# One pool of eight PSUM banks, three score groups in a run, and new step orders in a ragged attention kernel

## The chip, the cores and the metric

The kernel runs on one core of a Trainium2 chip. The metric is the device time in microseconds (us) of one execution. The core has five engines with a queue each: TensorE (PE, matrix products; the load of its weights is listed as PEld), VectorE (DVE), ScalarE (ACT), GpSimd (POOL) and SyncE (SP, which issues the transfers here). The engines wait for each other through semaphores only. PE writes its products to PSUM, a memory of eight banks, each of 512 fp32 values on 128 partitions; DVE or ACT must read a bank out before PE may write it again.

## The reference

32 sequences of up to 512 rows; each has its own length, drawn between 64 and 511, and eight heads of 64.

```python
output = np.zeros_like(x)
for b in range(batch):
    seq_len = lengths[b]
    x_b = x[b, :seq_len].copy()
    qkv = np.matmul(x_b, w_qkv)
    q, k, v = np.split(qkv, 3, axis=-1)        # then 8 heads of 64
    scores = scale * np.matmul(q, k.transpose(0, 2, 1))
    attn = np.exp(scores - np.max(scores, axis=-1, keepdims=True))
    attn = attn / (np.sum(attn, axis=-1, keepdims=True) + 1e-08)
    output[b, :seq_len] = np.matmul(attn, v).transpose(1, 0, 2).reshape(seq_len, dim)
```

## The kernel before

A head sorts the 32 sequences on the chip by length, longest first, and projects the first one. Then come seven loops, for padded lengths N of 512, 448, 384, 320, 256, 192 and 128. A loop's iteration handles two sequences, called **positions** j = 0 and j = 1; each has its own set of buffers. In this draw the loops run 1, 1, 4, 2, 3, 3 and 2 iterations, so 2, 2, 8, 4, 6, 6 and 4 positions. The number n of row tiles of 128 is 4 for 512 and 448, 3 for 384 and 320, 2 for 256 and 192, 1 for 128.

A position does the attention of its own sequence and, between that, the projections of the sequence of the next position (buffer index `o = 1 - j`). The work is written as **steps**, and the string `ORDER[N]` (lines 201 to 211) is the program order of every engine:

- `S` is a run of score groups. A group (`scores`, line 885) is PE's products of K and Q for two heads, in the upper and lower 64 rows of the array, into two adjacent banks (line 901), and ACT's exp of both banks into an fp16 tile `et` (line 915). For n = 4 there are 16 groups, for n = 3 there are 12, for n = 2 four, for n = 1 one. PE's group is emitted as the op `s…`; the ACT ops of a run come behind all PE groups of the run.
- `Q`, `K`, `V` (lines 926 and 949): four matmuls of full 128 rows per bank (more and narrower ones for lengths that are no multiple of 128; for N = 192 and 256 one Q or K step covers two column blocks), then a copy to fp16 by DVE, or by ACT where the step has a star.
- `A` (line 961): the product of `et` and the values with a column of ones (line 974) into one bank, then three DVE instructions: reciprocal `R` (line 984), masking of the reciprocal `U` (line 987), division `O` into the output tile (line 995). The bank is free when `O` has read it. For n = 4 an `A` step covers one head, for n = 3 and n = 2 two heads, for n = 1 four.
- `P`: mask (DVE, line 806), casts of a later sequence (POOL), its load (SP). `L`: the column of ones (DVE). `X`: SP's transposing transfer of the cast sequence, which is read two positions later. The store comes at the end of each position.

Before the change the banks are in two sets. `s_bufs` has two pairs, used in turn by the score groups, so a run is of two groups at most: a third would wait for the exp of the first. `singles` has four banks, dealt out in rounds of four or three by `ring_of` (line 781) to the Q, K, V and A steps in the order of `ORDER`.

`plan_waits` (line 35) follows the ops in program order and derives each op's waits from what it reads and writes (`bk3`, `ps0`, `et1` and so on). An order or a bank that is changed thus changes the waits; it needs no other edit. A wait stands ahead of its instruction in its engine's queue, and holds what is behind it.

Of the kernel before, what the change touches and what calls it, by code (L numbers as in the profile page):

```python
# [17 lines left out]
P = 128  # L18
# [16 lines left out]
def plan_waits(head, bodies, entries):  # L35
# [11 lines left out]


    waits = defaultdict(list)
    has = [{op.name for j in range(2) for op in body[j]} for body in bodies]  # L50
    shared = set().union(*has)

    def follow(chain):
# [4 lines left out]
        for at, v in enumerate(chain):  # L58
# [10 lines left out]
            for w, j, k, op in todo:  # L69
# [8 lines left out]
                for r in op.writes:  # L78
                    needs += [(o, False) for o in readers[r]]
                    needs += [(write[r], False)] if r in write else []  # L80
                for wait in waits[w, j, k]:
                    got = [
                        o
                        for o in seen[wait[1]]
                        if wait[0] in ("last", "entry", "head", "lead")
                        or (wait[0] == "pos" and o["b"] == b - wait[2])
                        or (wait[0] == "iter" and o["b"] // 2 == b // 2 - wait[2])
                        or (wait[0] == "posin" and o["b"] == first - wait[2])
                        or (wait[0] == "iterin" and o["b"] // 2 == first // 2 - wait[2])
                    ]  # L90
                    if got:
                        learn(got[-1])
# [53 lines left out]
def kernel(  # L146
# [25 lines left out]
    def ring(n, shape, dtype, name, pool=const):  # L172
# [11 lines left out]
    e_bufs = ring(4, [P, 2 * NT * MAXS], F16, "et")  # L184
    r_bufs = ring(4, [P, 2 * NT], FP32, "rcp")
    zeros = const.tile([P, NT - 1, D], FP32)
    order_i = const.tile([P, B + 8], I32)
    alive = const.tile([P, B + 8, NT], FP32)

    s_bufs = ring(2, [P, 2 * BANK], FP32, "psc", pool=ps)  # L190
    singles = ring(4, [P, BANK], FP32, "bank", pool=ps)

# [6 lines left out]
    LOOPS = [512, 448, 384, 320, 256, 192, 128]  # L199

    ORDER = {
        512: "P L S0 K2* Q1 S1 V0 K0 S2 A0 K1 S3 Q3* A1 S4 Q0 K3 S5 V3* Q2 S6 A2 A3 V2 S7 V1 X A4 "
        "A5 A6 A7",
        448: "P L S0 Q0 V3 S1 Q1* K0 S2 K2 V0 S3 K3 Q2 S4 A0 A1 A2 S5 K1 Q3 S6 A3 A4 A5 S7 V2 V1 X "
        "A6 A7",
        384: "P L S0 K0 V0* S1 V1 Q0* S2 A0 V2* S3 Q1 K1* A2 S4 Q2 Q3 S5 A4 K3 K2* X A6",
        320: "P L S0 K0* V0* S1 Q1 V1 S2 A0 V2 S3 A2 K1 Q0 S4 Q2* Q3* S5 A4 K3* K2* X A6",
        256: "P L V1* V0 S0 Q0* Q2 A0 S1 K2 A2 A4 K0* X A6",
        192: "P L S0 V0* V1 K0 S1 Q2 A0 Q0* A2 A4 K2* X A6",
        128: "P L S0 K0* Q0 V0 X A0 A4",  # L210
# [57 lines left out]
    def before_loops():  # L268
# [146 lines left out]
        hit_i = hit("hit_i", idx_f, idc_f, ("idx_f", "idc_f"))  # L415
        sorted_i = spread("phit_i", hit_i, singles[2], "bk2", 0)
        hit_l = hit("hit_l", idx_f, lenc_f, ("idx_f", "lenc_f"))
        sorted_l = spread("phit_l", hit_l, singles[1], "bk1", 0)
        op(
# [44 lines left out]
        back_l = hit("back_l", idr_f, lenc_f, ("idr_f", "lenc_f"))  # L464
        mirrored_i = spread("pback_i", back_i, singles[3], "bk3", 0)
        mirrored_l = spread("pback_l", back_l, singles[3], "bk3", B)

# [113 lines left out]
        def cast_tile(b, t, eng):  # L581
# [7 lines left out]

        where = {f"bk{k}": singles[k] for k in range(4)}  # L590
        where |= {
            f"ps{k}.{h}": s_bufs[k][:, h * BANK : (h + 1) * BANK] for k in range(2) for h in range(2)
        }

# [45 lines left out]
        def warm():  # L640
            for k in range(WARM):
                nc.tensor.matmul(where["ps1.1"][:, 0:P], ident16, ident16, start=True, stop=True)

        op("warm", "PE", warm, ("ident16",), ("ps1.1",))
        cast_tile(0, 0, "DVE")
        cast_tile(0, 1, "ACT")
        turn(0, 0, "ps0.0", "DVE")
        turn(0, 1, "ps0.1", "ACT")
        cast_tile(0, 2, "DVE")
        cast_tile(0, 3, "POOL")  # L650
        step("V0", "bk0", "DVE")
        turn(0, 2, "ps1.0", "DVE")
        shorten("wq", w_q, 0, 0, "ACT")
        step("V1", "bk1", "DVE")
        turn(0, 3, "ps1.1", "ACT")
        shorten("wq", w_q, 0, 1, "POOL")
        step("V2", "ps0.0", "DVE")
        shorten("wq", w_q, 0, 2, "ACT")
        step("V3", "ps0.1", "ACT")
        shorten("wq", w_q, 0, 3, "POOL")  # L660
# [12 lines left out]
        cast_tile(1, 2, "POOL")  # L673
        step("Q3", "ps1.0", "ACT")
        op(
# [45 lines left out]
        read_ends("PE", 1)  # L721
        step("K0", "ps1.1", "DVE")
        cast_tile(1, 1, "DVE")
        step("K1", "bk0", "ACT")
        cast_tile(1, 3, "ACT")
# [17 lines left out]
        )  # L743
        step("K2", "bk1", "DVE")
        for t, (bank, eng) in enumerate(
            (("ps0.0", "DVE"), ("ps0.1", "ACT"), ("ps1.0", "DVE"), ("ps1.1", "ACT"))
        ):
            turn(1, t, bank, eng)
# [31 lines left out]

    def ring_of(count):

        threes = -count % 4
        rounds = [3] * threes + [4] * ((count - 3 * threes) // 4)
        return [k for r in rounds for k in range(r)]

    def position(N, j, at, ring):
# [97 lines left out]
        def scores(g):  # L885
            group = groups[g]
            buf = g % 2 if len(groups) > 1 else j
            psc, W = s_bufs[buf], len(group) * n128
            i0, kt0 = group[0]
# [6 lines left out]
            def matmuls():  # L896
                for x, (i, kt) in enumerate(group):
                    for par in range(2):
                        r = slice(HD * par, HD * (par + 1))
                        c0 = par * BANK + x * n128  # L900
                        last = nc.tensor.matmul(  # L901
                            psc[:, c0 : c0 + N],
                            kT[r, i, kt * P : (kt + 1) * P],
                            qz[r, i, 0:N],
                            start=True,
                            stop=True,
                        )
                return last

            def exps():  # L910
                et = e_bufs[e][:, used : used + 2 * W].rearrange(
                    "p (j x q) -> p j x q", j=2, q=n128
                )
                got = psc.rearrange("p (j c) -> p j c", c=BANK)[:, :, 0:W]
                return nc.scalar.activation(  # L915
# [6 lines left out]
            reads = {f"kT{j}.{i}" for i, _ in group} | {f"qz{j}.{i}" for i, _ in group}  # L922
            op(f"s{g}", "PE", matmuls, (*sorted(reads), f"kTd{j}"), (f"ps{buf}",))
            return Op(f"S{g}", "ACT", exps, (f"ps{buf}",), (f"et{e}",))

        def qk(name, m0, is_q, act):
            k = ring.pop(0)
            bank = singles[k]
            ms = slice(m0, m0 + gm)
# [19 lines left out]
        def val(name, t, act):  # L949
            k = ring.pop(0)  # L950
            bank = singles[k]

# [8 lines left out]
        def av(h0):  # L961
            k = ring.pop(0)
            pav = singles[k][:, 0 : heads * n * (HD + 1)].rearrange(
                "p (g t d) -> p g t d", t=n, d=HD + 1
# [52 lines left out]
        for step in ORDER[N].split():  # L1017
# [10 lines left out]
            elif kind == "S":  # L1028
                run = [scores(g) for g in range(2 * num, min(2 * num + 2, len(groups)))]
                ops.extend(run)  # L1030
# [38 lines left out]
    for N in LOOPS:  # L1069
        steps = [s for s in ORDER[N].split() if s[0] in "QKVA"]  # L1070
        ring = ring_of(2 * len(steps))
        bodies.append([position(N, j, at, ring) for j in range(2)])
# [181 lines left out]
```

## Time and profile before

| | us |
|---|---|
| median of 3 runs (362.82, 363.5, 363.8) | 363.5 |
| the profiled execution's own time | 364.13 |
| its span, first to last instruction | 362.3 |
| PE busy in the span | 347.1 (96%) |
| ACT busy | 269.3 (74%) |
| DVE busy | 220.1 (61%) |

By stage, from the trace: where each loop's first PE instruction starts, and how long it lasts.

| stage | from | to | us | positions |
|---|---|---|---|---|
| head | 0 | 24.0 | 24.0 | |
| 512 | 24.0 | 63.4 | 39.4 | 2 |
| 448 | 63.4 | 99.8 | 36.4 | 2 |
| 384 | 99.8 | 205.4 | 105.6 | 8 |
| 320 | 205.4 | 254.0 | 48.6 | 4 |
| 256 | 254.0 | 300.3 | 46.3 | 6 |
| 192 | 300.3 | 340.9 | 40.6 | 6 |
| 128 | 340.9 | 362.3 | 21.4 | 4 |

In the profile's lines, a group is given by line, engine and operation, with output and inputs by the program's names. Behind the bar stand its busy time and the mean duration of one, then the idle time of the engine ahead of it, with what ended it. Matmuls overlap, so the mean duration of one is longer than the distance from one to the next. `issue` means that nothing which the profile shows was waited for.

### The profile page before, as it was taken

To read this page: it belongs to the slowest core of one execution; us is meant where nothing else is said; L and a number is where in the kernel's file an instruction comes from. 1 tells how busy PE (TensorE), PEld (TensorE's weight loads), DVE (VectorE), ACT (ScalarE), POOL (GpSimd) and SP (SyncE) were. 2 spreads that over 40 slices of the span, in tenths; PEclk is the share of its full clock that TensorE was granted. 3 is DMA by queue.
4 is the path that set the end of the run, shared out by engine and by line. 5 is a ranking of instruction groups with operands and counts; after the bars stand their busy time and mean duration, and the time that the engine had idled before them with its cause. 6 is when DMAs were issued, how large, how long until landed. Compare 5 with 4: busy or idle time off the path is not lost.

```text
span 362.3 us, 11181 instructions
## 1 busy us (share of the span) xinstructions
PE 347.1 (96%) x4274; PEld 216.1 (60%) x4274; DVE 220.1 (61%) x679; ACT 269.3 (74%) x390; POOL 96.6 (27%) x117
## 2 busy tenths in 40 slices
PE   4999999999999999999999999999999999999983
PEld 3444545474645555555555676677667777787762
DVE  4465656686856545645645666445665667667674
ACT  4379797878788898898898887888667776676541
POOL 4474040404033033033023023311223222322321
PEclk9999999999999999999999999999999999999998
DMA  5978971577169276376466469484786585875821
GB/s 202 346 255 246 261 261 24 171 277 238 55 209 299 89 225 238 103 257 197 121 243 206 128 237 249 133 267 153 239 183 213 192 250 161 259 246 185 235 75 59
DMA packets 74140, 72.35 MB, mean 200 GB/s; under 512 B 44160, under 2 KB 44160, under 8 KB 74112
## 3 DMA queue, kind: packets, MB, share of 16 engines
q1 hardware_dynamic: 74064, 71.98, 62.5%
q8 instruction: 17, 0.28, 0.3%
q14 instruction: 11, 0.09, 0.1%
q10 hardware_dynamic: 48, 0.00, 0.0%
HBM read 27.80 MB, written 33.55 MB: 169 GB/s over the span
## 4 chain that ended last, share of the span: by engine, by line
PE 91%; DMA 3%; SPq 2%; DVE 1%; issue 1%; ACT 0%
PE bank L219 39%; PE bank L230 19%; PE psc L901 16%; PE bank L974 16%; DMA w_q<-in_w_qkv_dram 2%; DMA xT<-x 1%; DMA row<-in_lengths_dram 1%; SPq L820 1%; PE psc L219 0%; SPq L487 0%; DVE v_aug L954 0%; SPq L845 0%; PE psc L230 0%; PE psc L600 0%; DVE out_nat L995 0%
## 5 line engine op out<-in xcount | busy, mean ns | idle before, releaser
L915 ACT ACTIVATE et<-psc 128x768 f16<-128x768 f32 (+3 forms) x260 | 208.4, 855 | 46.9 <-PE psc L901 46.6
L219 PE MATMUL bank<-xT,w_r 128*128 128x384 f16 (+4 forms) x1432 | 157.2, 258 | 1.4 <-DMA xT<-x 1.0
L257 POOL TENSOR_TENSOR x<-x_nat,mask 128x512 f16<-128x512 f32 x87 | 88.3, 1040 | 253.6 <-DVE mask L806 246.0
L219 PEld LDWEIGHTS bank<-xT,w_r 128*128 128x128 f16 x1432 | 99.2, 98 | 52.0 <-issue 18.7
L230 PE MATMUL bank<-w_r,xT 128*128 128x512 f16 x328 | 82.7, 382 | 0.3
L974 PEld LDWEIGHTS bank<-v_aug,et 128*128 128x128 f16 x1792 | 63.9, 98 | 14.1 <-issue 9.1
L974 PE MATMUL bank<-v_aug,et 128*128 128x65 f16 x1792 | 71.7, 194 | 0.0
L901 PE MATMUL psc<-qz,kT 64*128 64x384 f16 (+6 forms) x640 | 68.5, 306 | 1.0 <-ACT kT L939 1.0
L995 DVE TENSOR_TENSOR out_nat<-bank,rcp 128x256 f32<-128x256 f32 (+1 forms) x136 | 64.1, 472 | 4.6
L939 DVE CAST qz<-bank 128x384 f16<-128x384 f32 (+3 forms) x60 | 35.4, 591 | 40.6 <-PE bank L219 39.3
L984 DVE RECIPROCAL rcp<-bank 128x4 f32<-128x4 f32 (+1 forms) x136 | 24.7, 182 | 40.1 <-PE bank L974 40.0
L954 DVE CAST v_aug<-bank 128x512 f16<-128x512 f32 x46 | 31.8, 692 | 24.5 <-PE bank L230 24.3
L230 PEld LDWEIGHTS bank<-w_r,xT 128*128 128x128 f16 x328 | 27.8, 98 | 31.1 <-issue 6.8
L901 PEld LDWEIGHTS psc<-qz,kT 64*128 64x128 f16 x640 | 23.4, 93 | 33.1 <-issue 27.4
L939 ACT CAST kT<-bank 128x384 f16<-128x384 f32 (+2 forms) x46 | 23.1, 502 | 15.1 <-PE bank L219 15.1
L939 DVE CAST kT<-bank 128x384 f16<-128x384 f32 (+3 forms) x46 | 27.4, 595 | 7.7 <-PE bank L219 7.6
L987 DVE TENSOR_TENSOR rcp<-rcp,v_aug 128x4 f32<-128x4 f32 (+1 forms) x136 | 22.9, 169 | 4.7
L954 ACT CAST v_aug<-bank 128x512 f16<-128x512 f32 x34 | 20.0, 590 | 7.3 <-PE bank L230 6.7
L939 ACT CAST qz<-bank 128x384 f16<-128x384 f32 (+3 forms) x32 | 15.6, 502 | 2.5 <-PE bank L219 2.2
L806 DVE TENSOR_SCALAR mask<-alive 128x4 f32 x32 | 5.6, 175 | 5.7 <-issue 5.7
L869 DVE TENSOR_SCALAR v_aug<-alive 128x24 f16 (+3 forms) x32 | 7.2, 224 | 0.0
L409 PE MATMUL bank<-h_hit_i,h_ones 32*128 32x32 f16 x1 | 0.2, 204 | 4.3 <-DVE h_hit_i L392 4.3
(76 smaller groups left out, 54.9 us busy)
## 6 DMA issues: line engine op xcount, KB each, us to landing
x_nat<-in_x_dram SPq DMA_DIRECT2D x12, 768.0 KB, 4.7
out_dram<-out_nat SPq DMA_DIRECT2D x12, 768.0 KB, 3.5
x_nat<-in_x_dram SPq DMA_DIRECT2D x7, 1024.0 KB, 6.0
x_nat<-in_x_dram SPq DMA_DIRECT2D x13, 512.0 KB, 3.7
out_dram<-zeros SPq DMA_DIRECT2D x12, 512.0 KB, 5.7
out_dram<-out_nat SPq DMA_DIRECT2D x12, 512.0 KB, 3.2
out_dram<-out_nat SPq DMA_DIRECT2D x4, 1024.0 KB, 4.3
out_dram<-zeros SPq DMA_DIRECT2D x4, 768.0 KB, 8.4
```

Source lines behind the costliest of these rows:

```text
L219: last = nc.tensor.matmul(dst[:, t0 * P : t0 * P + (t1 - t0) * width], w_r[:, c, w0 : w0 + P], xT[:, t0:t1, c, 0:width], start=(c == 0), s ...
L230: last = nc.tensor.matmul(pv, xT[:, t, c, :], w_r[:, c, 2 * D : 3 * D], start=(c == 0), stop=(c == NC - 1),)
L257: return engine.tensor_tensor(out=x16, in0=x32, in1=live.broadcast_to([P, D]), op=ALU.mult)
L869: return nc.vector.tensor_scalar(out=v_bufs[o][:, 0:n, :, HD], in0=alive[:, bass.ds(at("DVE") + (j + 1), 1), 0:n] .rearrange("p o t -> p ( ...
L901: last = nc.tensor.matmul(psc[:, c0 : c0 + N], kT[r, i, kt * P : (kt + 1) * P], qz[r, i, 0:N], start=True, stop=True,)
L915: return nc.scalar.activation(out=et[:, :, :, 0:N], in_=got.rearrange("p j (x q) -> p j x q", q=n128)[:, :, :, 0:N], func=AF.Exp, scale=scale,
L939: return copy_on(act)(out=buf[:, ms, 0:N], in_=bank[:, 0 : gm * N].rearrange("p (m q) -> p m q", q=N),)
L954: return copy_on(act)(out=v_bufs[o][:, t, :, 0:HD], in_=bank.rearrange("p (h d) -> p h d", d=HD))
L974: last = nc.tensor.matmul(pav[:, g, qt, :], e_bufs[e][:, c0 + qt * P : c0 + (qt + 1) * P], v_aug[:, kt, h, :], start=(kt == 0), stop=(kt = ...
L984: return nc.vector.reciprocal(out=rcp, in_=pav[:, :, :, HD])
L987: return nc.vector.tensor_tensor(out=rcp, in0=rcp, in1=v_aug[:, 0:n, h0 : h0 + heads, HD].rearrange("p t g -> p g t"), op=ALU.mult,)
L995: return nc.vector.tensor_tensor(out=o_t[:, 0:n, h0 * HD : (h0 + heads) * HD].rearrange("p t (g d) -> p g t d", d=HD), in0=pav[:, :, :, 0:HD],
```

## The change

Four edits belong together.

1. The two sets of banks become one tile of eight banks. `allotted(N)` gives every step its bank, by a fixed rule that is worked out when the kernel is built: the banks are kept in order of their last use; a Q, K, V or A step takes the longest unused one; a score group takes the adjacent pair whose more recently used bank is oldest. It goes through both positions of a loop up to six times, until the order repeats, and keeps the last deal.
2. A run of scores has up to three groups for n = 4 and n = 3 (`RUN`), and two as before for n = 2. So a position has six runs (3, 3, 3, 3, 3, 1) in place of eight for n = 4, and four in place of six for n = 3.
3. `ORDER` is new for every length but 128. Steps change place, and stars move: some copies go from ACT to DVE and back.
4. Around it: eight reciprocal tiles in place of four, other bank names in the head, and one more dependency in `plan_waits`: an op waits for the last op of the same name, where that ran on another engine.

No matmul, exp, copy or transfer is added or removed.

```diff
-    r_bufs = ring(4, [P, 2 * NT], FP32, "rcp")
+    r_bufs = ring(8, [P, 2 * NT], FP32, "rcp")
...
-    s_bufs = ring(2, [P, 2 * BANK], FP32, "psc", pool=ps)
-    singles = ring(4, [P, BANK], FP32, "bank", pool=ps)
+    psum = ps.tile([P, 8, BANK], FP32, name="banks")
+    banks = [psum[:, k, :] for k in range(8)]
...
+    RUN = {4: 3, 3: 3, 2: 2, 1: 2}
     ORDER = {
-        512: "P L S0 K2* Q1 S1 V0 K0 S2 A0 K1 S3 Q3* A1 S4 Q0 K3 S5 V3* Q2 S6 A2 A3 V2 S7 V1 X A4 "
-        "A5 A6 A7",
-        448: "P L S0 Q0 V3 S1 Q1* K0 S2 K2 V0 S3 K3 Q2 S4 A0 A1 A2 S5 K1 Q3 S6 A3 A4 A5 S7 V2 V1 X "
-        "A6 A7",
-        384: "P L S0 K0 V0* S1 V1 Q0* S2 A0 V2* S3 Q1 K1* A2 S4 Q2 Q3 S5 A4 K3 K2* X A6",
-        320: "P L S0 K0* V0* S1 Q1 V1 S2 A0 V2 S3 A2 K1 Q0 S4 Q2* Q3* S5 A4 K3* K2* X A6",
-        256: "P L V1* V0 S0 Q0* Q2 A0 S1 K2 A2 A4 K0* X A6",
-        192: "P L S0 V0* V1 K0 S1 Q2 A0 Q0* A2 A4 K2* X A6",
+        512: "P L S0 V3 K3 Q2* S1 V2 K0 Q1 S2 Q3 K1* V0 S3 K2 A0 V1* S4 A1 Q0 X A2 S5 A3 A4 A5 A6 A7",
+        448: "P L S0 K3 K2 Q0 S1 V2 V3 A0 S2 V1 Q2 A1 S3 V0 K1 Q3* S4 K0 A2 A3 S5 Q1* X A4 A5 A6 A7",
+        384: "P L S0 Q0* K1 Q1 S1 Q3 V1 A0 S2 A2 V2 K0* S3 Q2 K2* K3* A4 A6 V0 X",
+        320: "P L S0 K2 Q1 K0 S1 V0 V2* A0 S2 K1* K3* A2 Q0* S3 Q3* A4 Q2* V1* X A6",
+        256: "P L V1* V0 S0 Q0 K2* S1 A0 K0* A2 A4 Q2* X A6",
+        192: "P L V0 S0 K0 S1 Q2 V1 A0 K2* A2 A4 A6 Q0* X",
         128: "P L S0 K0* Q0 V0 X A0 A4",
     }
...
+                needs += [(o, False) for o in seen[op.name][-1:] if o["by"] != op.eng and not op.dma]
...
-        step("K0", "ps1.1", "DVE")
+        step("K0", "bk1", "DVE")
...
-        step("K1", "bk0", "ACT")
+        step("K1", "bk2", "ACT")
...
-    def ring_of(count):
-
-        threes = -count % 4
-        rounds = [3] * threes + [4] * ((count - 3 * threes) // 4)
-        return [k for r in rounds for k in range(r)]
+    def runs(N):
+
+        groups = NH // 2 * tiles(N) // max(1, BANK // (tiles(N) * P))
+        return [min(RUN[tiles(N)], groups - k) for k in range(0, groups, RUN[tiles(N)])]
+
+    def allotted(N):
+
+
+        takes = []
+        for step in 2 * ORDER[N].split():
+            if step[0] == "S":
+                takes += [2] * runs(N)[int(step[1:])]
+            elif step[0] in "QKVA":
+                takes.append(1)
+        ages = list(range(8))
+        for _ in range(6):
+            before, got = list(ages), []
+            for n in takes:
+                first = ages[0]
+                if n == 2:
+                    first = min(
+                        range(7),
+                        key=lambda k: (
+                            max(ages.index(k), ages.index(k + 1)),
+                            ages.index(k) + ages.index(k + 1),
+                        ),
+                    )
+                got.append(first)
+                used = list(range(first, first + n))
+                ages = [k for k in ages if k not in used] + used
+            if ages == before:
+                break
+        return got
...
-            buf = g % 2 if len(groups) > 1 else j
-            psc, W = s_bufs[buf], len(group) * n128
+            k0 = ring.pop(0)
+            psc, W = [banks[k0], banks[k0 + 1]], len(group) * n128
...
-                got = psc.rearrange("p (j c) -> p j c", c=BANK)[:, :, 0:W]
+                got = psum[:, k0 : k0 + 2, 0:W]
...
-                run = [scores(g) for g in range(2 * num, min(2 * num + 2, len(groups)))]
+                first = sum(runs(N)[:num])
+                run = [scores(g) for g in range(first, first + runs(N)[num])]
```

## The prediction, made before the changed kernel ran

> **What bounds the kernel now.** I read the page first (busy shares, the chain that ended last), then the waits, then the list of groups by shape, then the timeline of the places that the change touches.
>
> ```profile
> PE 347.1 (96%) x4274; PEld 216.1 (60%) x4274; DVE 220.1 (61%) x679; ACT 269.3 (74%) x390; POOL 96.6 (27%) x117
> ...
> PE 91%; DMA 3%; SPq 2%; DVE 1%; issue 1%; ACT 0%
> ...
> PEld psc L901 <- issue: 27.4, 68, 0.6
> ...
> PEld bank L230 <- DVE out_nat L995: 0.8, 4, 0.2
> ...
> PEld bank L219 <- DVE v_aug L954: 0.7, 2, 0.4
> ```
>
> PE is the bound: 91% of the chain, and hardly a wait of PE's for a bank is listed (0.8 and 0.7 us). So time can be gained only by what PE itself does, and lost by every new wait of PE's.
>
> ```profile
> L219 PE MATMUL bank<-xT,w_r 128*128 128x384 f16 x320 | 61.2, 327 | 0.0
> ...
> L901 PE MATMUL psc<-qz,kT 64*128 64x384 f16 x192 | 23.9, 328 | 0.0
> ...
> 101.85 0.50 PE L901 MATMUL psc<-qz,kT 64*128 64x384 f16 x4
> ...
> 102.28 1.04 PE L230 MATMUL bank<-w_r,xT 128*128 128x512 f16 x4
> ```
>
> A position at N = 384 takes 13.20 us on PE (105.6 us of the stage by 8). Its blocks, start to start in the timeline: a Q or K 0.65, a V 0.865, an A 0.55. That is 8 x 0.65 + 3 x 0.865 + 4 x 0.55 = 10.0; the six runs of two groups get 3.2, or **0.535 a run**. Inside a run the second group comes 0.17 behind the first (a run is busy 23.9 / 48 = 0.50, one matmul lasts 0.33). So 2 x 0.17 of a run are its groups, and about 0.2 is paid at its two ends: the block ahead takes 0.10 longer than elsewhere (0.96 against 0.865 for the V ahead of the run at 101.85), and the run's last group 0.26 in place of 0.17. The waits show the same place: 27.4 us of weight loads of L901 that idle for nothing shown.
>
> **The change part by part.**
>
> *Longer runs.* A run of three costs 0.535 + 0.17 = 0.71, if the third group follows as the second does (bounds: 0.16, its columns alone, and 0.26, the last of a run; I take 0.17, the row of the same kind). Four such runs take 2.84 in place of 6 x 0.535 = 3.21: 0.37 less a position at N = 384. At 320 the same sum gives 0.36 (run of two 0.48, third group 0.145), at 448 and 512 about 0.39, as two of eight pairs of ends go. By itself: 8 x 0.37 + 4 x 0.36 + 4 x 0.39 = **6.0 us less**.
>
> *The bank waits that this buys.* I dealt out the banks by the rule and laid the blocks end to end, each with its readers on DVE and ACT behind it. In the middle of the positions the banks come back in time, narrowly: at 384, S1 and S2 find their banks free 0.2 to 0.5 before they ask, S3's last pair (A2 and V2 had it) 0.15. The end of a position is another matter. The reader of an A step is long, and DVE takes one at a time:
>
> ```profile
> 62.85 0.17 DVE L984 RECIPROCAL rcp<-bank 128x4 f32<-128x4 f32 x1
> ...
> 63.26 0.42 DVE L995 TENSOR_TENSOR out_nat<-bank,rcp 128x256 f32<-128x256 f32 x1
> ...
> 63.39 0.55 PE L901 MATMUL psc<-qz,kT 64*128 64x448 f16 x4
> ...
> 63.60 0.17 DVE L984 RECIPROCAL rcp<-bank 128x4 f32<-128x4 f32 x1
> ...
> 64.75 0.42 DVE L995 TENSOR_TENSOR out_nat<-bank,rcp 128x256 f32<-128x256 f32 x1
> ...
> 184.29 0.20 DVE L984 RECIPROCAL rcp<-bank 128x6 f32<-128x6 f32 x1 [1.04 <-PE bank L974]
> ...
> 184.73 0.56 DVE L995 TENSOR_TENSOR out_nat<-bank,rcp 128x384 f32<-128x384 f32 x1
> ```
>
> Reciprocals follow each other by 0.75 (62.85 to 63.60) while PE makes an A in 0.49, and the last of four ends at 65.18, 1.79 after PE began the next position at 63.39. Before, score groups had banks of their own and did not care. Now S0 takes six of eight banks at once, and the A steps at the end hold some of them.
>
> - **384, each position:** it ends A4 A6 V0, and S0's third pair is the banks of A4 and A6. From A4's start: its reciprocal at +0.76 (183.53 to 184.29), its division done at +1.75, A6's done at +2.66, free at +2.71. PE is at the next S0 after 2 x 0.55 + 0.865 + 0.095 = 2.06, at the third group after 2.41. Wait 0.30. Of 0.37 gained 0.07 to 0.08 is left: 8 x -0.08 = **-0.65**.
> - **448 to 384, once:** the loop's first deal does not know what the last loop left. S0's first pair is the bank of A6 (its division ends 1.04 after S0's nominal start, as at 64.43), the second that of A7 (+1.79). The third group then comes at 2.01 in place of 0.65: **+1.35**.
> - **512 and 448:** S0's second or third pair is A4's and A5's, and the first K or V takes A6's bank. 512 ends with five A steps behind a short S5, 448 with four. Laid out: 512 gains 0.55 in its first position (0.39, and a wait of 0.2 in S4 that the new order lacks); its second gains 0.55 and gives back 0.47; 448's first gives back 0.58 of 0.38, its second 0.3. **-0.65 and +0.1**.
> - **320:** ends V1* X A6, so only a Q1 waits for A6 (0.04) and Q3 for A2 (0.05): 4 x -0.27, +0.3 at its start for 384's A6, -0.2 at its end, where the last A6 stood 0.25 longer than others: **-0.95**.
> - **256 and 192**, runs of two as before. The 256 position is 7.72 a piece (46.3 / 6), its blocks make 7.49; the rest is a wait of V1 for A4's division (the row of L230 above), and the loop's end. New: V1's and V0's banks are A2's and A4's with Q2 and A6 in between, so it is gone, 0.1 to 0.2 a position; and 192 now opens with V0, which hides 256's last copies, where S0 waited 0.5. **-0.95** with 0.13 left at each loop end. At 192 (blocks 6.52, now 6.67) the wait of K2 for a bank goes (-0.15 each), but DVE gets one more copy (V0) and three A steps in a row: 3 x 0.75 behind A0's puts A6's division 1.6 into the next position, where, in every j = 0 but the first, S0's second group wants its bank at 1.14: 2 x +0.45. Its last position ends A6 Q0* in place of K2* A6, and the 128 loop's S0 needs that copy (340.90 is 0.93 behind K2's block), so A6's 0.25 no longer lies in that wait. **+0.2**.
> - **128:** K0 waited for V0's copy (344.85, 352.92: the row of L219). With eight banks it takes one long free; the first of the two is followed by a transfer's wait anyway (1.05 us at 349.31), the second is not: **-0.25**.
> - **Head:** K0 now uses Q2's bank, whose copy ends 0.05 after PE gets there (19.53): **+0.05**. The new dependency by name orders an op against one in an earlier loop, done tens of us before: 0, and below 0 is excluded.
> - **SP, POOL.** X comes later at 384 and 192 (behind the last block instead of ahead of A6) and earlier at 512. What it brings is read two positions later, so 6.5 us at least are there for its 1.3 to 1.6 of issue and 2.4 of transfer, also with the 1.5 us that SP was late at 334.75. The store behind it waits for the last division. POOL's casts hang on the mask behind it on DVE, up to 0.5 later, with 8 us spare. In the 512 stage, ACT's fullest (33.96 busy of 39.36), the new order has as many starred copies as the old, three. All at 0; if X's cover is gone, it costs once per position what it is late.
>
> Sum: 0.05 - 0.65 + 0.1 - 0.65 + 1.35 - 0.95 - 0.95 + 0.2 - 0.25 = **-1.75**. The profiled execution, 364.13 with a span of 362.3, lies 0.63 above the median, so its sum is 362.4; against the median, 363.5 - 1.75, about **361.8**. Bounds of this case: no wait at the ends of positions 512 to 320 and 0.1 less per third group would give 357.5; half a wait more in each n = 3 and n = 4 position (0.15 x 16) 364.1.
>
> **The rivals.**
>
> *The banks are free in time: the whole gain comes.* Then each position is its blocks: 384 -3.0, 512 and 448 -1.9, 320 -1.65, 256 -1.0, 192 -0.65, 128 -0.25, in all -8.5: **355.0**. For it: the old PE has next to no bank waits. Against it: DVE's 0.75 and 0.9 per A are measured, and the deal puts S0 on those banks.
>
> *ACT becomes late, slower than before.* ACT must do three exps behind each other (0.71 apart at 384, 0.92 at 512), and copies with a star stand behind them; the next run's banks hang on those copies. At 512, S3.2 takes K1*'s bank with 0.08 to spare and S4.1 follows S3.2's exp with none; at 320, S3.2 takes K1*'s and K3*'s with 0.13. If ACT is one exp later than I laid out, 512 and 448 pay 0.9 and 0.8 per position, 320 pays 0.5: 1.8 + 1.6 + 1.9 = 5.3 on top of -1.75, **367.0**; it decides for slower from 2.8 us, half an exp. For it: ACT is busy 86% of the 512 and 85% of the 384 stage. Against it: 14% are free, and PE gets slower with every wait. The Trainium skill ("TensorEngine Tiling (Array Packing)", PSUM Bottleneck) warns that packing the array speeds up TensorE but not the emptying of PSUM, so that the copies may become the bottleneck. By that rule the gain of longer runs is lost to evacuation; the trace agrees so far that the readers (ACT 86%, DVE's 0.75 per A) are the near limits.
>
> *The ends are paid per group, not per run.* Then the third groups return 16 x 0.37 and nothing is gained: **367.7**. Against it: the second group of a run follows in 0.17.
>
> **How the numbers follow.** Forecast 0.5 (360.0 to 363.6), full gain 0.17, ACT late 0.25 (363 to 367), per group 0.08. 0.3%, 1.1 us, is about what can be told from no change. Faster (below 362.4): 0.5 x 0.75 + 0.17 + a little of ACT late = 0.57. Slower (above 364.6): 0.25 x 0.65 + 0.08 + a little = 0.25. Same: 0.18. The range, 357.5 to 365.8, leaves out most of the full gain below and the worse half of a late ACT above; the forecast's own is 360.0 to 363.6.
>
> **What would show it.** Right: PE's waits list bank and psc loads that wait for DVE out_nat L995, about 0.3 x 8 at 384 and over 1 us once at the start of that stage; the L901 idle put to issue falls by a quarter; a 384 position takes 13.1, a 320 position 11.85, a 256 position 7.5. Wrong: no waits for out_nat (full gain), waits of L901 for ACT et or ACT copies (ACT late), a third group that starts over 0.3 behind the second.

## The result, and the profile after

The changed kernel takes 364.81 us (median of 8 runs, 364.25 to 365.95), the kernel before 363.41 beside it (8 runs, 362.82 to 363.8): a ratio of 1.0044, 95% interval 1.003 to 1.0057. By the ratio it is slower by 0.44%, 1.6 us (the medians lie 1.4 apart); forecast was 361.8. The profiled execution took 364.5, with a span of 362.7.

The page of the changed kernel, busy times and the chain that ended last:

```profile
PE 341.9 (94%) x4274; PEld 215.9 (60%) x4274; DVE 222.4 (61%) x681; ACT 263.8 (73%) x388; POOL 96.6 (27%) x117
...
PE 78%; DVE 12%; DMA 3%; issue 2%; SPq 2%; ACT 1%; POOL 1%; POOLq 0%
```

PE itself is busy 5.2 us less (347.1 before), close to the 6.0 that the longer runs were to save. But the chain now runs through VectorE for 12% of the span, where it was 1%.

The waits of PE and of its weight loads in the changed kernel (line 926 are the scores, 220 and 231 the projections; in us in total, times, longest):

```profile
PEld banks L926 <- issue: 16.9, 46, 0.7
...
PEld banks L926 <- DVE out_nat L1021: 7.9, 14, 1.1
...
PEld banks L926 <- ACT qz L965: 3.4, 7, 0.7
PEld banks L220 <- DVE out_nat L1021: 2.9, 7, 0.7
PEld banks L1000 <- DVE v_aug L980: 2.5, 8, 0.3
...
PE banks L231 <- DVE out_nat L1021: 1.5, 2, 1.2
```

The idle time at the ends of the runs ("issue") fell from 27.4 to 16.9. New are the waits for the divisions (`out_nat`, line 1021), which hardly existed before. The row of ScalarE's copies (`qz`, line 965) is the sign that the forecast gave for a late ScalarE; five of its seven waits, 0.42 each, stand in the loop of 192, whose positions take 6.51 all the same (forecast 6.52).

By stage, from the first score matmul of a loop to that of the next, in both traces; the forecast's terms are put to the same boundaries (a wait ahead of a loop's first scores belongs to the stage before it, and 256 and 192 are taken together because the first V moved across their border):

| stage | before | after | change | forecast | beyond the forecast |
|---|---|---|---|---|---|
| 512 | 39.36 | 38.93 | -0.43 | -0.65 | +0.22 |
| 448, and the first wait of 384 | 36.41 | 37.86 | +1.45 | +1.15 | +0.30 |
| 384, and the first wait of 320 | 105.60 | 106.22 | +0.62 | -0.05 | +0.67 |
| 320, and the start of 256 | 50.41 | 49.91 | -0.50 | -1.25 | +0.75 |
| 256 and 192 | 85.09 | 85.27 | +0.18 | -0.75 | +0.93 |
| 128 and the end | 21.4 | 21.4 | 0.0 | -0.25 | +0.25 |
| sum | | | +1.32 | -1.80 | +3.12 |

The head is left out: its length varies between executions of one kernel (the first scores start at 23.0 to 24.8 in the traces below), and it was 0.92 shorter in this one.

Where it was as forecast, the timeline of the changed kernel at the end of a position of 384 shows it (start, duration, engine, line and operation; in brackets the engine's idle time ahead, and what ended it):

```profile
112.50 0.56 DVE L1021 TENSOR_TENSOR out_nat<-banks,rcp 128x384 f32<-128x384 f32 x1
...
113.38 0.97 PE L926 MATMUL banks<-qz,kT 64*128 64x384 f16 x6
113.40 0.56 DVE L1021 TENSOR_TENSOR out_nat<-banks,rcp 128x384 f32<-128x384 f32 x1
...
114.01 0.10 PEld L926 LDWEIGHTS banks<-qz,kT 64*128 64x128 f16 x2 [0.52 <-DVE out_nat L1021]
```

The run of three is busy 0.97 where an undisturbed one is busy 0.66: its third group stands behind A6's division, which ends at 113.96, 0.90 behind A4's. That is the forecast's wait of 0.30, and it comes in each position. A position takes 13.16; forecast was 13.12.

Where it was not, the largest place is the entry of the loop of 192:

```profile
299.99 0.42 DVE L1021 TENSOR_TENSOR out_nat<-banks,rcp 128x256 f32<-128x256 f32 x1
...
300.56 1.02 PE L231 MATMUL banks<-w_r,xT 128*128 128x512 f16 x4 [1.16 <-DVE out_nat L1021]
```

V0, 192's first step, waits 1.16 for the last division of 256. The forecast had this V0 as the cover for 256's last copies and put no wait ahead of it.

### The profile page after: what moved, and what is told of

It reads as the page before. It is cut to its first block, busy times and chain, and to the rows that moved or that the text cites. A ratio compares the mean times of both kernels' runs of the same rounds, so it can differ in the third digit from the quotient of the medians.

```text
span 362.7 us, 11162 instructions
## 1 busy us (share of the span) xinstructions
PE 341.9 (94%) x4274; PEld 215.9 (60%) x4274; DVE 222.4 (61%) x681; ACT 263.8 (73%) x388; POOL 96.6 (27%) x117
## 4 chain that ended last, share of the span: by engine, by line
PE 78%; DVE 12%; DMA 3%; issue 2%; SPq 2%; ACT 1%; POOL 1%; POOLq 0%
PE banks L220 36%; PE banks L231 17%; PE banks L926 14%; PE banks L1000 11%; DVE out_nat L1021 6%; DVE rcp L1013 2%; DVE rcp L1010 2%; DMA w_q<-in_w_qkv_dram 2%; ACT et L940 1%; DMA xT<-x 1%; DVE v_aug L980 1%; DMA row<-in_lengths_dram 1%; SPq L846 1%; POOL w_r L575 1%; SPq L488 0%
## 5 line engine op out<-in xcount | busy, mean ns | idle before, releaser
L940 ACT ACTIVATE et<-banks 128x768 f16<-128x768 f32 (+3 forms) x260 | 204.1, 856 | 52.1 <-PE banks L926 51.9
L220 PE MATMUL banks<-xT,w_r 128*128 128x256 f16 (+4 forms) x1440 | 157.7, 259 | 2.3 <-DMA xT<-x 1.5
L220 PEld LDWEIGHTS banks<-xT,w_r 128*128 128x128 f16 x1440 | 101.1, 98 | 51.8 <-issue 13.3
L231 PE MATMUL banks<-w_r,xT 128*128 128x512 f16 x336 | 84.7, 380 | 2.0 <-DVE out_nat L1021 1.5
L1000 PEld LDWEIGHTS banks<-v_aug,et 128*128 128x128 f16 x1792 | 63.8, 98 | 13.8 <-DVE v_aug L980 2.5
L926 PE MATMUL banks<-qz,kT 64*128 64x384 f16 (+6 forms) x640 | 65.1, 305 | 4.7 <-DVE out_nat L1021 2.2
L1000 PE MATMUL banks<-v_aug,et 128*128 128x65 f16 x1792 | 69.4, 194 | 0.0
L1021 DVE TENSOR_TENSOR out_nat<-banks,rcp 128x256 f32<-128x256 f32 (+1 forms) x136 | 64.1, 472 | 4.6
L980 DVE CAST v_aug<-banks 128x512 f16<-128x512 f32 x64 | 44.3, 692 | 24.5 <-PE banks L231 24.4
L965 DVE CAST qz<-banks 128x384 f16<-128x384 f32 (+3 forms) x54 | 32.2, 597 | 31.7 <-PE banks L220 30.0
L926 PEld LDWEIGHTS banks<-qz,kT 64*128 64x128 f16 x640 | 23.1, 94 | 35.9 <-issue 16.9
```

Of the source, the lines that this page charges most:

```text
L220: last = nc.tensor.matmul(dst[:, t0 * P : t0 * P + (t1 - t0) * width], w_r[:, c, w0 : w0 + P], xT[:, t0:t1, c, 0:width], start=(c == 0), s ...
L231: last = nc.tensor.matmul(pv, xT[:, t, c, :], w_r[:, c, 2 * D : 3 * D], start=(c == 0), stop=(c == NC - 1),)
L926: last = nc.tensor.matmul(psc[par][:, x * n128 : x * n128 + N], kT[r, i, kt * P : (kt + 1) * P], qz[r, i, 0:N], start=True, stop=True,)
L940: return nc.scalar.activation(out=et[:, :, :, 0:N], in_=got.rearrange("p j (x q) -> p j x q", q=n128)[:, :, :, 0:N], func=AF.Exp, scale=scale,
L965: return copy_on(act)(out=buf[:, ms, 0:N], in_=bank[:, 0 : gm * N].rearrange("p (m q) -> p m q", q=N),)
L980: return copy_on(act)(out=v_bufs[o][:, t, :, 0:HD], in_=bank.rearrange("p (h d) -> p h d", d=HD))
```

## The experiments

Theory A: the longer runs save what was forecast, and it is given back to late divisions, within the positions and at the entries of the loops. Rivals: the entries' waits are real and can't be had otherwise; the pool costs by itself; VectorE's work costs either kernel alike.

**e1: a loop waits only for the loop just ahead.** `plan_waits` gives the first steps of a loop the waits of every loop that could stand ahead of it, by the steps' names. A bank that 448 held last in A6 makes a wait for "the division of the last A6", and if 256 stands ahead, that is 256's A6, whichever bank it had.

```diff
-        follow(["head", v, v])
-        for u in range(v):
-            follow([u, v, v])
+        if v == 0:
+            follow(["head", v, v])
+        else:
+            follow([v - 1, v, v])
```

> The changed kernel, with one edit in plan_waits: a loop's first waits are worked out from the loop right before it alone (the head for the first loop), not from every loop that could stand before it. In this draw every loop runs, so these are the waits that the data needs. Theory A (the entry of a loop waits for the division of a step of the same name, A6, that in the loop actually before used another bank): the wait of 1.33 us ahead of 192's first V0 falls to about 0.2, the one ahead of 320's first S0 from 0.64 to some 0.3 in all, the one inside 256's first two V steps (0.18) goes; the one ahead of 384 (1.67, S0 and its second group) stays, since 448's own A6 and A7 hold those banks. In all -1.7 us: 363.1 against 364.8, ratio to before 0.999 to 1.000. Theory B (the loop entries cost what the engines' branches and registers cost, whatever the banks): no change, 364.8.

364.04, ratio 1.0008 (0.9997 to 1.0019), against 1.0044 for the changed kernel: 1.3 us less, of the 1.7 that theory A gave. In the trace the stage of 384 with 320's first wait is 0.66 shorter, that of 256 0.80, all stages together 1.4. Timeline of e1 at 192's entry:

```profile
300.83 1.04 PE L232 MATMUL banks<-w_r,xT 128*128 128x512 f16 x4 [0.43 <-ACT qz L966]
300.99 0.42 DVE L1022 TENSOR_TENSOR out_nat<-banks,rcp 128x256 f32<-128x256 f32 x1
```

V0 now begins before the division that it had waited for. So that wait was for no bank of V0's: 1.3 us of the 3.1 beyond the forecast are waits by name. By the deal the 0.43 that V0 still waits, for a copy of ScalarE, is by name as well: V0's bank was last held in 256 by a score group, but by Q2 where 192 stands behind 192, and e1 leaves that chain in. No run takes it out.

**e2: A4 earlier in the position of 384.**

```diff
-        384: "P L S0 Q0* K1 Q1 S1 Q3 V1 A0 S2 A2 V2 K0* S3 Q2 K2* K3* A4 A6 V0 X",
+        384: "P L S0 Q0* K1 Q1 S1 Q3 V1 A0 S2 A2 V2 K0* S3 Q2 A4 K2* K3* A6 V0 X",
```

> The changed kernel, and in the order of 384 alone A4 goes two steps ahead: Q2 A4 K2* K3* A6 V0 in place of Q2 K2* K3* A4 A6 V0. The same blocks and the same four runs of three. Theory A (VectorE's reciprocal, mask and division of A6 stand behind those of A4, and S0 wants A6's bank too early): with A4 1.3 us earlier, A6's reciprocal starts as soon as PE is done, its division ends 0.36 earlier, S0's second wait of 0.30 goes to about 0, a 384 position falls from 13.16 to 12.86, in all -2.2 us: 362.6, ratio 0.998. Theory C (ScalarE's exps or starred copies are late, or the third group is slow): the order of two A steps changes nothing of that, 364.8; if the exps were the limit, A6 would wait for them as before.

362.34, ratio 0.9963 (0.9948 to 0.9979). The stage of 384 takes 103.78 in place of 106.22. Timeline of e2 at the same place:

```profile
114.52 0.56 DVE L1021 TENSOR_TENSOR out_nat<-banks,rcp 128x384 f32<-128x384 f32 x1
...
114.85 0.66 PE L926 MATMUL banks<-qz,kT 64*128 64x384 f16 x6
```

The run is busy 0.66 again. With A4 and A6 two K steps apart, A6's reciprocal no longer queues behind A4's division on VectorE. One step moved by two places makes the kernel faster than the one before.

**e3 and e5: without the mask step.** Both leave out `U`, the product of a tile's reciprocals with its mask, so the output isn't masked; e3 from the changed kernel, e5 from the kernel before.

```diff
-            op(f"U{h0}", "DVE", only_live, (f"r{k}", f"vl{j}"), (f"r{k}",))
```

> The changed kernel without U, the instruction that masks the reciprocal: rows beyond a sequence's length are not set to zero. It takes 0.17 of some 0.75 (n = 4, 2) or 0.9 us (n = 3) off each A step's work on VectorE, 0.2 with its gap, and nothing off PE or ScalarE. Theory A (PE waits for divisions at the ends of positions and at the loops' entries): 384 loses 0.30 and 0.06 a position (-2.8), 512 and 448 about -1.2, 320 about -1.0, 192 -0.9, the entries about -1.5, in all -7: about 357.5, ratio 0.984. Theory C (ScalarE or the runs themselves): VectorE's work lies beside PE's, no more than -0.5: 364.3.

> The kernel before without the step U (the product of a tile's reciprocals with its mask on VectorE); its output is not masked, so this part of the computation is left out. It is the control of e3, where the same removal made the changed kernel 8.3 us faster. Theory A (the changed kernel lost its gain to divisions that end late, because its matmuls wait for them; before's matmuls hardly waited for a division): little to gain here, 362.4 to 363.6, a ratio of 0.997 to 1.000. Rival D (U's time on VectorE costs either kernel the same, and e3 says nothing of the change): as in e3, about 355.5, a ratio of 0.98.

e3: 356.49, ratio 0.9806 (0.9787 to 0.9825), 8.3 us less than the changed kernel. e5: 361.44, ratio 0.994 (0.9924 to 0.9957), 2.3 less than the kernel before. In e5 the stages of 512, 448, 384 and 320 keep their length to 0.03 us; what it gains lies in the loops of 256, 192 and 128, 0.3, 1.0 and 0.4, where I had expected next to nothing. In e3 the four long stages lose 0.55, 1.54, 3.35 and 1.13. So VectorE's chain sets PE's pace in the long loops of the changed kernel alone. With the step gone from both, the ratio of e3 to e5 is 0.9806 / 0.994 = 0.987, 4.9 us for the change.

**e4 and e6: the pool alone.** Both have the new pool and rule with the old orders and runs of two; e6 has e1's edit too.

```diff
-    RUN = {4: 3, 3: 3, 2: 2, 1: 2}
+    RUN = {4: 2, 3: 2, 2: 2, 1: 2}
```

> One part alone: the old orders and runs of two, with all eight banks dealt out by the new rule (and the new dependency by name). Theory A (the pool costs only where three pairs are wanted at once and the last A steps hold them): a run of two takes four of eight banks, so S0 finds four older ones; the old kernel's own bank waits (256, 192, 128: about 1.5 us) go, and some 1 to 2 us of entry waits for a division come in; 362 to 364.5, ratio 0.996 to 1.003. Theory D (a shared pool is worse by itself, since scores now wait for what Q, K, V and A steps leave behind): PE waits in every position, 365 or more.

> The new pool and rule with the old orders and runs of two (e4), and the edit of e1: a loop's first steps wait only for what the loop just ahead of it last held in their banks. In e4 the pool alone cost 3.8 us, nearly all of it at the entries of the loops. Theory A1 (the entries pay for waits that stand for loops further back and fall by name on late steps of the loop just ahead): most of that goes, 363.6 to 365.0, a ratio of 1.000 to 1.004. Theory A2 (the entries pay because the banks that a loop starts with are truly those that the loop just ahead holds last, as its deal starts anew): nothing or little goes, 366.5 to 367.6, a ratio of 1.008 to 1.011.

e4: 367.42, ratio 1.0107 (1.0087 to 1.0127), a clear miss; nothing that I had laid out lets the pool cost 3.8 us. The time is theory D's, its mechanism (waits in every position) is not. e6: 365.22, ratio 1.0044 (1.0027 to 1.006). The positions of 384 in e4 are as long as before (13.2), and yet PE waits, in the list of waits of e4:

```profile
PE banks L928 <- DVE out_nat L1023: 5.5, 6, 1.4
...
PEld banks L928 <- DVE out_nat L1023: 3.7, 4, 1.5
```

The two rows mostly count the same waits, once on PE and once on its weight loads. All stand at the entries of five loops (448, 384, 320, 192 and 128), up to 1.4 us each on PE, and none inside a later position. 448 takes 39.27 in place of 36.41. e6 lies just above what theory A1 gave: 2.3 us of e4's 3.8 are waits by name, 1.5 are something else.

**e9 and e12: where the pool's price lies.** e9 is e6 with another first age of the banks, the order of last use that a loop's deal starts from, in the five longest loops (`ages = list(FIRST[N])` in place of `list(range(8))`). e12 is e9 with one more edit of `plan_waits`, valid where 448 runs one iteration:

```diff
+        if v == 1:
+            follow([v - 1, v])
+            continue
         follow([v, v, v])
```

> The kernel of e6 (new pool and rule, old orders, runs of two, waits of the loop just ahead) with one more edit: the deal of each of the loops of 512, 448, 384, 320 and 256 starts from another age of the banks, chosen so that the banks that a loop asks for first are not those that the loop ahead releases last. Steps, orders and runs are those of e6. Theory A2 (what is left of the pool's price, 1.0044 in e6, is paid at the entries of 448 and 384, because each loop's first deal starts from a fixed age of the banks): those two waits of 1.3 and 1.4 us go, 362.0 to 363.0, a ratio of 0.996 to 0.999, so the pool by itself costs nothing. Rival F (a pool of eight shared banks costs time by itself, since score groups now wait for the readers of single banks): as e6, 365.2, a ratio of 1.004.

> The kernel of e9 with one edit in the plan of waits: the loop of 448, which runs one iteration in this draw, takes its waits only from the chain that really happens (512, then 448 once), not also from the chain 448 after 448. In e9 its S0 waits 1.14 and 0.65 for the divisions of A6 and A7 of the loop of 512, because in 448 after 448 its banks would be those of 448's A6 and A7; in truth they are A4's and A5's. Theory A2', what e9 left: the entry pays for a holder that doesn't exist in this run. By the rows of e9 (divisions end at 63.14, 63.88, 64.63; PE is ready at 63.60) S0 then waits 0.0 and 0.13 and K0 0.45 for A6's bank, 1.1 us less than e9: 363.2 to 363.9, a ratio of 0.998 to 1.000. Rival F (the pool costs by itself): as e9, a ratio of 1.002.

e9: 364.63, ratio 1.0023 (1.0009 to 1.0038), between the two theories. The timeline of e9 at 448's entry tells why:

```profile
64.21 0.42 DVE L1033 TENSOR_TENSOR out_nat<-banks,rcp 128x256 f32<-128x256 f32 x1
...
64.69 0.36 PE L938 MATMUL banks<-qz,kT 64*128 64x448 f16 x2 [1.02 <-DVE out_nat L1033]
...
64.95 0.42 DVE L1033 TENSOR_TENSOR out_nat<-banks,rcp 128x256 f32<-128x256 f32 x1
...
65.43 0.36 PE L938 MATMUL banks<-qz,kT 64*128 64x448 f16 x2 [0.38 <-DVE out_nat L1033]
```

S0's first groups wait for the divisions of 512's A6 and A7 (they end at 64.63 and 65.37). By the deal their banks were A4's and A5's. The waits come from the chain of 448 behind 448, in which A6 and A7 do hold those banks; it never happens here, as the loop runs once, but the wait is by name and catches 512's. e12, which leaves that chain out:

```profile
63.90 0.42 DVE L1036 TENSOR_TENSOR out_nat<-banks,rcp 128x256 f32<-128x256 f32 x1
...
64.04 0.71 PE L941 MATMUL banks<-qz,kT 64*128 64x448 f16 x4
...
64.65 0.42 DVE L1036 TENSOR_TENSOR out_nat<-banks,rcp 128x256 f32<-128x256 f32 x1
...
65.13 0.94 PE L235 MATMUL banks<-xT,w_r 128*128 128x384 f16 x8 [0.38 <-DVE out_nat L1036]
```

363.46, ratio 0.9999 (0.999 to 1.0008). The first row is A5's division, the last A6's: the scores start ahead of A6's, and 1.1 us of the stage is gone. So the pool by itself costs nothing on balance: 448's first position still takes 0.6 longer than before (18.81 against 18.21), and the loops of 256, 192 and 128 take 1.4 less. Its price in e4 was paid at the loops' entries, to waits by name and to a first deal that gives the banks released last.

**e10: the changed kernel with another first age.** e1 with another first age for 384 and 256; no order is changed.

> The kernel of e1 (the changed kernel, waits of the loop just ahead) with another first age of the banks in the loops of 384 and 256 alone; orders and runs are the changed kernel's. At 384 the deal then repeats in another way, in which S0's third pair is no longer the banks of A4 and A6. Theory A (the position's wait of 0.30 comes from which banks the deal gives, not from the order of the steps): a position of 384 takes 12.85 in place of 13.16, 2.1 us less over its eight positions bar the first; 320's entry may wait up to 0.95 for a bank of V0 in place of 0.65 at most now. In all 1.5 to 2.1 less than e1: 362.0 to 362.6, a ratio of 0.995 to 0.9975. If the wait follows the order of the steps (A4 A6 V0 at the end) whatever the deal: 364.0, a ratio of 1.001.

363.04, ratio 0.9971 (0.9951 to 0.9991), by the ratio in the range that theory A gave, by the time 0.4 above it. S0 of a 384 position is busy 0.66 although A6's division runs beside it, so the wait hung on the banks and not on the order of the steps. A position takes 12.98 and not the 12.85 that I gave: small waits came up at other steps. The entry of 320 now waits 0.88 for the copy of V0, near the 0.95 given.

**e7: e2 and e1 together.**

> The changed kernel with both A4 ahead of K2* and K3* in the loop of three tiles (e2, 2.4 us faster than the changed kernel) and the edit of e1 (0.8 us faster than it). The two act at different places, the positions of that loop and the entries of the later loops, so theory A expects the sum: 362.3 less 0.8 to 1.3, 361.0 to 361.5, a ratio of 0.993 to 0.995. If the entry of the loop of two tiles, where e2 left more to wait for, takes the gain back: 362.3, a ratio of 0.996.

361.37, ratio 0.9942 (0.9926 to 0.9959). The two gains add up: they are waits at different places.

**e8: orders and first ages for the divisions.** All six longer loops get a new order and a first age, chosen by laying the blocks end to end with their readers, as the prediction did, and moving steps until the banks came in time; plus e1's edit. Two of the orders:

```diff
+        384: "P L K0 S0 V1* K3 Q3 S1 V2* K2 Q2 S2 Q0 V0* A0 S3 A2 Q1* A4 K1* X A6",
+        320: "P L K2* K0 S0 K3 Q3 K1 S1 A0 V1 S2 A2 V2* Q2* S3 Q0* Q1 A4 V0* X A6",
...
-        ages = list(range(8))
+        ages = list(FIRST[N])
```

> The changed kernel's pool, rule and longer runs, with the edit of e1, and with other orders and another first age of the banks in each of the six longer loops, both chosen so that within a loop the bank that a matmul step takes was released well before (an A step's division, a copy of ScalarE). Theory A (the waits within the positions are what the longer runs' gain of 6.0 us went to): the changed kernel's waits for out_nat (7.9, 2.9, 2.2 and 1.5 us by its rows), for v_aug (2.5) and for qz (3.4) fall to those of the loops' entries, some 5 us in all, so 354 to 358, a ratio of 0.974 to 0.985. Rival E (what is gained within the positions is given back at the entries, since each loop's first deal takes no notice of what the loop ahead left: the pool alone cost 3.8 us there): 360 to 364, a ratio of 0.99 to 1.00.

358.94, ratio 0.9883 (0.9859 to 0.9907): better than rival E, short of theory A. Within the loops theory A held for the divisions. From 512's first scores to 128's it takes 310.1 in place of 318.2, and PE's waits for divisions are down to these, in the list of waits of e8:

```profile
PEld banks L241 <- DVE out_nat L1031: 2.2, 7, 0.3
...
PEld banks L230 <- DVE out_nat L1031: 0.4, 1, 0.4
```

Theory A let the waits for `v_aug` fall too; they stay at 2.5 us, behind ScalarE in place of VectorE. And from 128's first scores to the end it takes 23.6 in place of 21.4. The timeline of e8 in the loop of 128:

```profile
334.67 1.04 POOL L268 TENSOR_TENSOR x<-x_nat,mask 128x512 f16<-128x512 f32 x1 [4.73 <-DVE mask L842]
...
340.26 1.24 SPq L881 DMA_TRANSPOSE xT<-x  x1
...
342.73 2.52 PE L230 MATMUL banks<-xT,w_r 128*128 128x128 f16 x32 [2.18 <-DMA xT<-x]
```

And three stretches of the windows of e8 (us, busy time and instructions of PE, PEld, DVE, ACT and POOL, granted clock of PE, DMA share, GB/s):

```profile
342.00:343.50 1.50, 0.77 (x14) 0.78 (x15) 0.51 (x3) 0.00 (x0) 0.68 (x1) 1.00 0.27 98
343.50:345.00 1.50, 1.50 (x22) 1.50 (x20) 0.00 (x0) 0.59 (x1) 0.36 (x1) 0.65 0.36 138
345.00:346.50 1.50, 1.50 (x7) 0.65 (x5) 0.69 (x1) 0.00 (x0) 0.00 (x0) 0.50 0.31 117
```

The first row is the cast that the transfer reads. The wait for the transfer is 0.65 longer than in the changed kernel, and behind it the granted clock is 0.50 for 3.4 us (343.94 to 347.35), in which a Q takes 1.41 in place of 0.89 and a V 1.71 in place of 0.86.

**e11: the mask of the loop of 128 on ScalarE.** e8, with that mask made by ScalarE, to bring the cast and the transfer forward.

```diff
+            if n == 1:
+                return nc.scalar.copy(
+                    out=m_bufs[o],
+                    in_=alive[:, bass.ds(at("ACT") + (j + 3), 1), :].rearrange("p o t -> p (o t)"),
+                )
...
-                op("M", "DVE", pair_mask, (), (f"m{o}",))
+                op("M", "ACT" if n == 1 else "DVE", pair_mask, (), (f"m{o}",))
```

> The kernel of e8 with the mask of the loop of one tile made by ScalarE in place of VectorE, so that the cast and the transfer behind it start some 3 us earlier. In e8's third position of that loop PE waits 2.35 us for the transfer of xT, and the granted clock is 0.50 in the 3 us behind that wait: K0's block is not longer, but Q0's takes 1.41 in place of 0.89 and V0's 1.71 in place of 0.86. Theory G (the clock falls because PE stood still for over 2 us; in the changed kernel the same wait was 1.6 and the clock stayed): both go, 2.2 to 2.35 for the wait and 1.4 for the clock, 355.0 to 355.6, a ratio of 0.977 to 0.979. If the clock falls there for another reason (time since the start, the load before): the wait alone, 356.6, a ratio of 0.982. If the transfer is late for another reason than the mask: 358.9, a ratio of 0.988.

357.27, ratio 0.9825 (0.9795 to 0.9855), between the theories, and for none of their reasons. Timeline of e11:

```profile
333.27 1.04 POOL L268 TENSOR_TENSOR x<-x_nat,mask 128x512 f16<-128x512 f32 x1 [3.59 <-ACT mask L843]
...
333.45 1.24 SPq L886 DMA_TRANSPOSE xT<-x  x1
...
339.99 1.24 SPq L886 DMA_TRANSPOSE xT<-x  x1
...
342.45 1.96 PE L230 MATMUL banks<-xT,w_r 128*128 128x128 f16 x32 [2.18 <-DMA xT<-x]
```

The cast that the transfer reads is 1.4 us earlier than in e8, done at 334.31, and the transfer is issued at 339.99 all the same, 6.54 behind the one ahead of it. PE waits as long as in e8. So the transfer doesn't hang on the mask. e8's own rows show it too: its cast was done at 335.71, 4.5 us ahead of the transfer, so the edit had nothing to bring forward. And with the same wait the clock stays at 1.00, which is the whole gain: the loop of 128 takes 22.0 in place of 23.6. Theory G falls, at least as the whole cause. The mean granted clock was 0.989 to 0.991 in all four runs of e8 and 0.994 to 0.995 in those of e11. The two ran on different chips, so whether the chip or the edit makes the difference stays open. Of the versions that do the whole computation e11 is the fastest, 1.75% below the kernel before.

## Why the prediction was wrong, step by step

- **Longer runs, 6.0 us less: right.** The third group starts 0.16 behind the second at 384 and 0.14 at 320 (0.17 and 0.145 taken), PE is busy 5.2 us less, the idle time put to issue falls by 10.5 of 27.4 (a quarter was forecast). Where A6's wait is gone (e2) a position of 384 takes 12.84, 0.36 less than before; 0.37 was forecast. "The ends are paid per group" is out.
- **384, each position, 0.07 to 0.08 left of 0.37: right in mechanism, short in size.** The wait for A6's division is the 0.30 given; V2 waits another 0.06 for A0's, which I had not seen. A position of 13.16 in place of 13.12 makes 0.3.
- **448 to 384, 1.35 and 0.30: right.** PE loses 1.05 ahead of S0 and 0.62 inside it, 1.67. Here the banks' true holders, 448's own A6 and A7, are also those that the plan waits for, and e1 leaves this wait as it is.
- **The entries of 320, 256 and 192: the step that failed.** For 320 I put "+0.3 at its start", and it is 0.64 (0.38, inside S0, in e1: the true holder's part was sized right); for the start of 256 a gain of 0.2, and it is a loss of about 0.2; for 192 "now opens with V0, which hides 256's last copies", and V0 waits 1.16. I had dealt out the banks and asked who really held them. The waits don't come from that alone: `plan_waits` joins the waits of all loops that could stand ahead, by name. e1 shows 1.3 us of this; e4, e6, e9 and e12 show it for the pool alone. The forecast has no term for it. Its "new dependency by name", put at 0, is another thing: the joining stood in the kernel before too, and e1 cuts it down and leaves the new dependency in.
- **512 and 448, -0.65 and +0.1: right for the first positions** (19.03 and 18.36 against 19.13 and 18.41), **wrong for the second** (19.9 and 18.46, where the terms give 19.59 and 18.12). There S4's third group waits 0.25 and 0.30 for a copy of ScalarE, because the second position's deal gives it the bank of the V1* or Q3* just ahead of the run. I had laid out only the ends of the second positions. Together 0.5 us.
- **320, -0.27 a position:** it is -0.18. Three waits of some 0.08 (for A6, A0 and A2) where I had two of half that, 0.36 in all four.
- **256 and 192:** positions of 7.49 and 6.51 and the wait of 0.48 in each j = 0 of 192 but the first were as forecast (7.49, 6.52, 0.45). Only the entry between them was not.
- **128, -0.25:** K0's waits for V0's copy went, 0.27 twice, but the wait for the transfer behind them grew from 1.1 to 1.6. The transfer comes at SP's pace (last section), so PE's gain ahead of it is not kept.
- **The rivals.** The full gain never came near. "ACT becomes late" named the right kind and, in the main, the wrong engine: ScalarE's copies are 0.5 us of what lies beyond the forecast (the second positions of 512 and 448) and the 0.43 at 192's entry, VectorE's divisions most of the rest. The Trainium skill ("TensorEngine Tiling (Array Packing)", PSUM Bottleneck) says that packing speeds up the matrix engine but not the emptying of PSUM; e3 and e5 agree, with VectorE as the side that empties too slowly: 0.2 less per A step is worth 8.3 us after the change and 2.3 before it. I had put that rule under the rival of a late ScalarE.

Added up, +3.1 beyond the forecast: 0.5 for the second positions, 0.7 for small waits inside 384 and 320, the rest at the entries and in front of SP's transfer. The sign was wrong, and the forecast's own range (360.0 to 363.6) does not hold 364.8. That the whole range (357.5 to 365.8) does is luck: it reaches so far up for a late ScalarE.

## What to carry to other kernels

A shared pool of buffers joins what separate sets kept apart. Its price stands at the seams between loops, so lay out each seam, and take the waits from what the program will really wait on (names, counts, every chain it provides for), not from who holds the buffer. Where a late reader gives back a gain, look at the readers in a row: moving one of two A steps apart (e2) or starting the deal from another age (e10, with e1's edit) returned more than the whole loss, with the same work.

## What the runs showed of the hardware that I had not expected

SP has a pace of its own here: the last transpose of the loop of 192 and the only one of the loop of 128 are issued 6.51 to 6.54 us apart in the traces of all fourteen kernels, whatever PE, VectorE or the cast do. In between lie one store and steps of SP that the timeline does not list. The timeline of the kernel before:

```profile
340.33 1.24 SPq L845 DMA_TRANSPOSE xT<-x  x1
...
346.87 1.24 SPq L845 DMA_TRANSPOSE xT<-x  x1
```

And that of the changed kernel:

```profile
340.92 1.24 SPq L871 DMA_TRANSPOSE xT<-x  x1
...
347.45 1.24 SPq L871 DMA_TRANSPOSE xT<-x  x1
```

With 2.4 from issue to landing the second sequence is there 8.95 us behind the first issue. PE wants it 7.4 behind that issue in the changed kernel and 6.8 in e8 (340.48 - 333.72), so it waits 1.6 and 2.2: what PE gains between that first issue and this point, it loses there. The second finding is the clock of 0.50 for 3.4 us behind a pause of PE of 2.2 us in e8, which the equal pause in e11 did not bring. The Trainium skill ("TensorE: Matmul & The Clock Gate", Part 1: The HAM clock gate) says that the clock has two states, full and half, and falls to half after an idle window of about 3.4 us that runs freely. The depth and the length agree with e8's rows; the pause was shorter than that window, and a window that runs freely alone would hardly separate four runs of e8 from four of e11. The cause is open.
